# A two-layer diffusion backbone on one core: alternating block order, resident rope tables, and work moved between stages

## The chip, the cores and the metric

The kernel runs on 1 core of one Trainium2 chip. The metric is the device time of one execution in microseconds (us), lower is better. The time before is 1805.17 us, the median of 3 runs (1799.14 to 1805.18).

## The reference, cut to what matters

1024 latent tokens of width 1024 pass through two layers and a last RMSNorm, with 256 context tokens as extra keys; everything is float32.

```python
# layer 0: windowed attention, 16 query heads, 4 key/value heads of 128
shift, scale, gate = split(silu(c) @ ada_w[0] + ada_b[0], 3)
h = rmsnorm(x, norm_g[0]) * (1 + scale) + shift
q, k, v, z = split(h @ attn_w_in)            # 16 q, 4 k, 4 v, 16 z columns blocks of 128
q, k = rope(q, cos, sin), rope(k, cos, sin)
o = softmax([sink, q kc^T, masked q k^T]) @ [vc, v]   # |i-j| <= 128, and all 256 context keys
x = x + gate * ((o * silu(z)) @ attn_w_out)
# layer 1: convolution module, width 2048
shift, scale, gate = split(silu(c) @ ada_w[1] + ada_b[1], 3)
h = rmsnorm(x, norm_g[1]) * (1 + scale) + shift
a, gl, z = split(h @ conv_w_in + conv_b_in, 3)
u = depthwise_conv31(a * sigmoid(gl)) + conv_dw_b
x = x + gate * ((silu(layernorm(u)) * silu(z)) @ conv_w_out)
out = rmsnorm(x) * final_g
```

## The kernel before, in words

Every float32 product is made of three fast matmuls: each operand is split into a rounded high part (a copy on ScalarE) and a low part (the difference, `split_lo`, on VectorE or GpSimd), and high x high, high x low and low x high are added up. On chip, big tiles live in 44 pages of 128 x 1024 floats (`pg`) and 6 half pages (`hp`); `hx` hands out half pages, from `hp` first and then from `pg`. A page that is freed goes to the end of a queue and is handed out again in that order; whoever writes it next waits for its last reader, DMAs among them.

The stages, with their times in the profile:

- **Start (0 to 78 us).** Modulation of layer 0, the normalized input (`Hh`, `Hl`: high and low, 8 tiles of 128 x 1024 each), first projections.
- **Attention (78 to 930 us).** 128 steps, one for each head and block of 128 queries. A step issues the scores of the next step (`scores`), then `fill(n)`, then `pv` when one is queued, then `transposes`. TensorE works in program order. `fill` puts projection matmuls between the softmax steps so that TensorE has work while VectorE, ScalarE and GpSimd make the softmax; `quota(h, qb)` is the running count of such matmuls at each step (`HEAD0` for head 0, then sums for groups of heads). Small steps that follow a matmul are put off by a number of such matmuls (`soon(n, fn)`).
- The fill consists of the gate of head 0 (`job_gate`), context keys and values (`job_ctx`), and **pairs** (`job_pair`): two columns of weights of 128 (for instance q and z of one head) times all 1024 tokens, by the seven products of the Strassen-Winograd scheme in place of eight, each product 12 matmuls of 512 columns, 84 a pair, 18 pairs. `PairStream` loads a pair's two weight blocks, makes their sums and splits them, two products ahead. `sums` makes the sums of the input once (S1 to S4). S4 and S3 stay on chip; S1 and S2 are written to device memory (`sd`) and streamed back in each pair, four tiles of 512 KB each (`stream`, `hdone`). The pair stream has 11 pages of its own (`PW`). A pair's results need `finish`: rope for q and k (`rope_late`: two DMAs swap the halves of the head, and cosine and sine tables are loaded from device memory each time), the gate for z, a transpose for v.
- In the same steps run two jobs by the way. `ada_rest` makes the gate of layer 0 and all of layer 1's modulation: 16 chunks of 256 columns, 8 multiply-adds of 128 x 256 on VectorE each, the weights loaded 128 KB at a time into two buffers (`dww_raw`, `wsum_raw`), the sum kept beside the mask (`mask_page`). `low_parts` loads `conv_w_out` in 32 pieces, makes the low parts on ScalarE and GpSimd, and stores them (`wolC`).
- **Attention's output projection (930 to 1080 us)**, `proj_attn`: its weights are loaded, copied on ScalarE, and their low parts made on GpSimd; after each of its 32 steps `bgA` runs small jobs.
- **Convolution (1080 to 1585 us)**, and **last projection (1585 us to the end)**, `proj_out`: 32 steps of 24 matmuls; `w_load` loads the weight and its low part from `wolC`, `w_split` makes the high part. The second half of the layer norm runs between its steps (`bgB`).

Instruction order on VectorE, ScalarE, GpSimd and the DMA queue of SyncE (SP) is set by a planner outside the kernel from the dependencies and its own costs; each engine then works in that order.

Of the kernel before, what the change touches and what calls it, by code (L numbers as in the profile page):

```python
# [36 lines left out]
PW = 11  # L37
KEPT = 12
ROPE_AT = 12
HEAD0 = (30, 36, 36, 36, 36, 28, 28, 28)  # L40
# [109 lines left out]
def backbone_kernel(  # L150
# [185 lines left out]
    for key, src in (("k", 0), wk[0]), (("q", 0), wcol(0)), (("v", 0), wv[0]), (("z", 0), wcol(AW + 2 * KW)):  # L336
        add_chunk(key, src)
# [3 lines left out]
    wsA = WStream(chunks, nraw=4, lo_eng=lambda i: V if i < 4 or i % 2 else G)  # L341

    pairs = []
    for h in range(1, NH):
# [6 lines left out]

    pw = []

    class PairStream:
# [6 lines left out]
        def load(self):  # L361
            if self.nl >= 2 * len(pairs):
                return
            i, c = divmod(self.nl, 2)
            r = pw[0].alloc(F32, [2, 512], "wraw")
            SY.dma_start(out=r.rearrange("p a (b c) -> p (a b) c", c=P), in_=column(pairs[i][c]))
            self.raw[(i, c)] = r
            self.nl += 1

        def halves(self, src, i, b, then=None):  # L370
            t = pw[0].alloc(F32R, [2, 512], "whl")
# [10 lines left out]
        def split(self):  # L382
# [6 lines left out]
            r1, r2 = self.raw.get((i, 0)), self.raw[(i, 1)]  # L389

            def drop(c):
                pw[0].free(self.raw.pop((i, c)))
                self.load()

            if b == 0:
                self.halves(r1[:, 0], i, b)
                self.t[i] = t = pw[0].alloc(F32, [2, 512], "wt")
                tt(V, t[:, 0], r2[:, 1], r2[:, 0], ALU.subtract)
            elif b == 1:
                t = self.t[i]  # L400
                self.halves(t[:, 0], i, b)
                tt(V, r2[:, 0], r2[:, 0], r1[:, 0], ALU.subtract)
                tt(V, t[:, 1], r2[:, 1], r2[:, 0], ALU.subtract)
            elif b == 2:
                self.halves(r1[:, 1], i, b)
                tt(V, r1[:, 0], r1[:, 1], self.t[i][:, 1], ALU.subtract)
            elif b == 3:
                t = self.t.pop(i)
                self.halves(t[:, 1], i, b, lambda: pw[0].free(t))
            elif b == 4:  # L410
                self.halves(r1[:, 0], i, b, lambda: drop(0))
            elif b == 5:
                self.halves(r2[:, 1], i, b)
            else:
                self.halves(r2[:, 0], i, b, lambda: drop(1))
# [9 lines left out]
        def done(self, n):  # L425
            pw[0].free(self.hl.pop(n))
# [376 lines left out]

    def ada_rest():
        todo = [(l, c0) for l, c0 in [(0, 2048 + 256 * i) for i in range(4)] + [(1, 256 * i) for i in range(12)]]
        todo = [(l, c0, kt) for l, c0 in todo for kt in range(KT)]

        def load(i):
            l, c0, kt = todo[i]
            SY.dma_start(out=ada_raw[i % 2], in_=ada_w[l, kt * P:(kt + 1) * P, c0:c0 + 256])  # L810
# [3 lines left out]
        for i, (l, c0, kt) in enumerate(todo):  # L814
# [3 lines left out]
            if kt == 0:  # L818
                after(V.tensor_scalar(out=acc, in0=raw, scalar1=cs[:, kt:kt + 1], scalar2=None, op0=ALU.mult))
                for b in range(2):  # L820
                    col = (c0 - 2048 if l == 0 else 1024 + c0) // P + b
                    bs = slice(b * P, b * P + P)
                    stt(acc[:, bs], ident, abt[:, col:col + 1], acc[:, bs], ALU.mult, ALU.add)
            else:
                after(stt(acc, raw, cs[:, kt:kt + 1], acc, ALU.mult, ALU.add))
            yield "sum" if kt == KT - 1 else None
# [3 lines left out]
            if c0 >= 2048:  # L830
                PE.matmul(o[0:1, 0:256], ones[:, 0:1], acc_a, start=True, stop=True)
                row = hx.alloc("grow")
                V.tensor_copy(row[0:1, 0:256], o[0:1, 0:256])
                SY.dma_start(out=gd[l][:, c0 - 2048:c0 - 1792], in_=row[0:1, 0:256])
                soon(2 * KEPT, lambda row=row: hx.free(row))
            else:
                for b in range(2):
                    PE.matmul(o[:, b:b + 1], acc_a[:, b * P:b * P + P], ones[:, 0:1], start=True, stop=True)
                V.tensor_copy(mod1[:, c0 // P:c0 // P + 2], o[:, 0:2])
            yield  # L840

# [6 lines left out]
    wolC = dr.tile([2, NK, P, 2, 512], F32, tag="wolC", name="wolC")  # L848

# [3 lines left out]

    def low_parts():

        his = hx.alloc("lhi")
        hi = his.bitcast(F32R)
        for m in range(2):
            for kk in range(NK):
                for b in range(2):  # L860
                    raw = hx.alloc("low")
                    SY.dma_start(out=raw, in_=pair_rows(Wp, m, kk)[:, b])
                    yield
                    after(act(hi, raw, AF.Copy), anchor_a)
                    after(split_lo(G, raw, raw, hi), anchor_p)
                    yield
                    SY.dma_start(out=wolC[m, kk][:, b], in_=raw)
                    soon(KEPT, lambda raw=raw: hx.free(raw))
                    yield
        hx.free(his)  # L870
# [169 lines left out]
    def early_proj():  # L1040
        pg.free(*Hh, *Hl, *s4)
# [38 lines left out]
    def rope_late(e, half, d, then, queue):  # L1080
# [14 lines left out]
        def high_low():  # L1095
            hx.free(w, ct, st)
# [4 lines left out]
        def low(hi, lo):  # L1101
            split_lo(G, lo, e, hi)
            soon(KEPT, lambda: hx.free(e))
            if then:
# [5 lines left out]
    def rope(o, half, d, ropes=None, e=None, then=None):  # L1110
        sl = slice(half * 512, half * 512 + 512)
        if e is not None:
            return rope_late(e, half, d, then, SY)
        e = hx.alloc("rope")
        act(e, o, AF.Copy)
        if soon_on[0]:
            return rope_late(e, half, d, then, A)
# [36 lines left out]
    def finish(kind, n, half, o, d=None, ropes=None, e=None):  # L1154
# [7 lines left out]
        if kind in "qk":  # L1162
# [3 lines left out]
            rope(o, half, d, ropes, e, then)  # L1166
# [65 lines left out]
    def job_gate():  # L1232
        i = cidx[("z", 0)]
        wc = wsA.need(i)
        for half in range(2):
            o = ps_g()
            yield from gemm_half(wc, half, o)
            wsA.load()
            wsA.split()
            finish("z", 0, half, o)  # L1240
        wsA.done(i)
        for k in range(4):
            drive(sums(k), 1 + S_EVERY * k)
# [5 lines left out]
    def job_ctx(kind, g):  # L1249
        i = cidx[(kind, g)]  # L1250
        wc = wsA.need(i)
        wsA.load()
        o = ps_g()
# [14 lines left out]
        if (kind, g) == ("v", NG - 1):  # L1268
            for c in Hc:
                pg.free(*c)  # L1270
            pw.append(pg.part(PW))
            for _ in range(2):
                wsP.load()
            wsP.ahead(1)
            for k in range(4):
                stream(0, k)

    s4, win, ready = [], {}, set()
    ORDER = ("A11", "S3", "A12", "S2", "A22", "S4", "S1")
    STREAM = ("S2", "S1")  # L1280

    def sums(k):

        f, g = (pg.alloc(F32, [2, 512], "sf") for _ in range(2))
        for t, i, eng in ((f, k, V), (g, k + 4, G)):
# [7 lines left out]
        new = {n: pg.alloc(F32R, [2, 512], n) for n in ("S2", "S4", "S1")}  # L1293
        s4.append(new["S4"])
        dst = {n: (t[:, 0], t[:, 1]) for n, t in new.items()}
        dst["S3"] = Hh[k][:, 512:1024], Hl[k][:, 512:1024]
        for n, src in (("S3", f[:, 1]), ("S2", f[:, 0]), ("S4", g[:, 0]), ("S1", g[:, 1])):
# [1069 lines left out]
```

## Time and profile before

| what | value |
|---|---|
| median of 3 runs | 1805.17 us |
| the profiled execution, its own time | 1802.11 us |
| its span, first to last instruction | 1800.3 us |
| TensorE (PE) busy | 1682.3 us, 93% |
| VectorE (DVE) busy | 1374.4 us, 76% |
| GpSimd (POOL) busy | 1012.5 us, 56% |
| ScalarE (ACT) busy | 919.4 us, 51% |
| moved by DMA | 347.40 MB |

A matmul is counted as busy to its modelled end, and these overlap, so that a group's sum of durations is more than its share of the engine's time; the views by window count overlapped time once. Nearly all instructions go through short helper functions, so the line given (L144) says nothing; tiles are told by name. `name<-a,b` is written tile, read tiles. A name belongs to the first user of a half page, so `oz_page` or `sin_page` may hold another thing later.

### The profile page before, as it was taken

To read this page: it belongs to the slowest core of one execution; us is meant where nothing else is said; L and a number is where in the kernel's file an instruction comes from. 1 tells how busy PE (TensorE), PEld (TensorE's weight loads), DVE (VectorE), ACT (ScalarE), POOL (GpSimd) and SP (SyncE) were. 2 spreads that over 40 slices of the span, in tenths; PEclk is the share of its full clock that TensorE was granted. 3 is DMA by queue.
4 is the path that set the end of the run, shared out by engine and by line. 5 is a ranking of instruction groups with operands and counts; after the bars stand their busy time and mean duration, and the time that the engine had idled before them with its cause. 6 is when DMAs were issued, how large, how long until landed. Compare 5 with 4: busy or idle time off the path is not lost.

```text
span 1800.3 us, 24912 instructions
## 1 busy us (share of the span) xinstructions
PE 1682.3 (93%) x8221; PEld 1400.5 (78%) x8221; DVE 1374.4 (76%) x2337; ACT 919.4 (51%) x1649; POOL 1012.5 (56%) x778
## 2 busy tenths in 40 slices
PE   9986999978989989898889999999999999999998
PEld 6775777867778777776778888888888888878886
DVE  5995778976778777777832638999999999976833
ACT  6643554544455444444533435565656655466732
POOL 0464556654556555564634566799988998320300
PEclk9988999998999999999999999999999999999999
DMA  9457789966798779977645443110111112177891
GB/s 377 149 174 263 240 281 338 328 226 212 256 312 297 251 239 303 293 260 236 211 150 177 152 149 121 35 60 24 59 59 51 67 48 82 65 250 236 285 336 68
DMA packets 158498, 347.40 MB, mean 193 GB/s; under 512 B 16938, under 2 KB 43874, under 8 KB 158368
## 3 DMA queue, kind: packets, MB, share of 16 engines
q1 hardware_dynamic: 155168, 340.56, 56.2%
q10 hardware_dynamic: 3200, 5.25, 1.0%
q8 instruction: 65, 1.06, 0.2%
q14 instruction: 65, 0.53, 0.1%
HBM read 281.50 MB, written 53.75 MB: 186 GB/s over the span
## 4 chain that ended last, share of the span: by engine, by line
PE 62%; DVE 14%; DMA 13%; issue 4%; POOL 2%; ACT 2%; SPq 1%; ACTq 0%; DVEq 0%; POOLq 0%
PE psg L144 27%; PE pso L144 18%; PE pss L144 17%; DMA wraw_page<-in_k_win_dram 3%; DMA sw_page<-sd 2%; DVE mask_page L144 2%; DVE ptlo L144 2%; DVE p L144 2%; DVE sf_page L144 1%; DMA dww_raw<-in_ada_w_dram 1%; DMA rope_half<-rope_half 1%; DVE oz_page L144 1%; DMA wo_page<-in_attn_w_out_dram 1%; DVE wraw_page L144 1%; SPq L144 1%
## 5 line engine op out<-in xcount | busy, mean ns | idle before, releaser
L144 POOL TENSOR_TENSOR odd_half<-odd_half,prod_half 128x513 f32<-128x513 f32 (+2 forms) x252 | 315.8, 1261 | 27.4 <-ACT prod_half L144 14.4
L144 ACT ACTIVATE prod_half<-ubuf,dww 128x513 f32<-128x513 f32 (+2 forms) x252 | 167.1, 676 | 133.0 <-POOL odd_half L144 126.8
L144 POOL TENSOR_SCALAR p<-p,sc 128x640 f32<-128x640 f32 (+1 forms) x128 | 120.8, 944 | 188.7 <-DVE sc L144 122.6
L144 PE MATMUL psg<-hh_page,whl_page 128*128 128x512 f32 x576 | 193.4, 401 | 7.3 <-ACT oz_page L144 6.6
L144 PE MATMUL psg<-h2h_page,whi_page 128*128 128x512 f32 x464 | 181.8, 392 | 0.0
L144 PE MATMUL psg<-h2h_page,wlo_page 128*128 128x512 f32 x464 | 180.6, 389 | 0.0
L144 PE MATMUL psg<-h2l_page,whi_page 128*128 128x512 f32 x464 | 180.6, 389 | 0.0
L144 ACT ACTIVATE p<-p,sc 128x641 f32<-128x641 f32 (+1 forms) x128 | 102.9, 804 | 137.9 <-DVE sc L144 122.4
L144 DVE SCALAR_TENSOR_TENSOR pss<-ubuf,wsum,pss 128x512 f32<-128x512 f32 (+3 forms) x270 | 173.0, 676 | 0.3
L144 DVE SCALAR_TENSOR_TENSOR pss<-ubuf,dww,pss 128x512 f32<-128x512 f32 (+3 forms) x270 | 172.8, 676 | 0.2
L144 POOL TENSOR_TENSOR wlo_page<-wraw_page,whi_page 128x1024 fp32r<-128x1024 f32 (+1 forms) x38 | 88.8, 2341 | 115.0 <-ACT whi_page L144 77.6
L144 ACT ACTIVATE pthi<-pss 128x512 fp32r<-128x512 f32 (+2 forms) x144 | 86.7, 613 | 99.6 <-PE pss L144 94.2
L144 PEld LDWEIGHTS psg<-hh_page,whl_page 128*128 128x128 f32 x576 | 109.9, 194 | 29.0 <-ACT oz_page L144 7.0
L144 DVE TENSOR_TENSOR ptlo<-pss,pthi 128x512 fp32r<-128x512 f32 (+2 forms) x144 | 101.2, 712 | 30.6 <-ACT pthi L144 29.9
L144 ACT ACTIVATE woh_page<-wo_page 128x1024 fp32r<-128x1024 f32 x63 | 66.6, 1057 | 107.6 <-DMA wo_page<-in_conv_w_out_dram 44.8
L144 PE MATMUL pss<-kh_page,q_page 128*128 128x384 f32 (+1 forms) x256 | 97.8, 382 | 23.4 <-ACT q_page L144 9.8
L144 PE MATMUL pso<-h2h_page,whi_page 128*128 128x512 f32 x304 | 118.3, 389 | 0.0
L144 PE MATMUL pso<-h2l_page,whi_page 128*128 128x512 f32 x304 | 118.3, 389 | 0.0
L144 PE MATMUL pso<-h2h_page,wlo_page 128*128 128x512 f32 x304 | 118.3, 389 | 0.0
L144 PE MATMUL psg<-hl_page,whl_page 128*128 128x512 f32 x288 | 115.4, 401 | 0.0
L144 PE MATMUL pss<-ident,p 128*128 128x128 f32 x608 | 90.3, 278 | 22.8 <-DVE ptlo L144 11.2
L144 POOL TENSOR_TENSOR wol_page<-wo_page,woh_page 128x512 fp32r<-128x512 f32 x62 | 83.2, 1365 | 50.2 <-ACT woh_page L144 26.7
(536 smaller groups left out, 4714.7 us busy)
## 6 DMA issues: line engine op xcount, KB each, us to landing
sw_page<-sd SPq DMA_DIRECT2D x144, 512.0 KB, 6.1
wraw_page<-in_k_wconv_dram SPq DMA_DIRECT2D x48, 512.0 KB, 3.2
wraw_page<-in_k_win_dram SPq DMA_DIRECT2D x46, 512.0 KB, 5.0
wo_page<-in_attn_w_out_dram SPq DMA_DIRECT2D x32, 512.0 KB, 5.6
wo_page<-in_conv_w_out_dram SPq DMA_DIRECT2D x32, 512.0 KB, 9.7
wol_page<-wolC SPq DMA_DIRECT2D x32, 512.0 KB, 5.7
araw_page<-in_k_ada_dram SPq DMA_DIRECT2D x16, 512.0 KB, 10.2
dww_raw<-in_ada_w_dram SPq DMA_DIRECT2D x64, 128.0 KB, 4.5
```

The costliest lines, as they stand in the source:

```text
L144: r = f(*a, **k)
```

## The change

- **Pairs.** The order of the seven products is S1, A11, S3, S2, A12, S4, A22 in pairs of even number and A22, A11, S3, S2, A12, S4, S1 in odd ones. The tile at the end of a pair stays for the start of the next, so that only one of the two streamed tiles is loaded a pair (`stream_in`, 16 matmuls after the start, and up to 24 later while four pages or fewer are free). S2 takes the place of A22 in `Hh`, `Hl`; A22 and S1 are stored to `sd`. The bank that ends the pair changes with the order, weight sums follow it. One of four result sums goes from VectorE to GpSimd.
- **Head 1.** Its q and z are no pair: they are computed whole (`job_whole`, 48 matmuls each), so that there are 17 pairs. `sums` starts in the middle of z of head 1.
- **Pages.** The 11 pages of the pair stream are no longer set apart.
- **Rope.** The tables `cos` and `sin` stay on chip (two pages); the loads in `rope_late` are gone.
- **Fill.** `QUOTA` gives the fill for each head. Before the scores of a half head, fill goes on until rope of that half q has ended (before: until the pair had got to q of that head).
- **Modulation.** `ada_rest` keeps the gate of layer 0 (4 of 16 chunks, a step in three). Layer 1's is made in `ada_last`, three small pieces after each step of attention's output projection: 48 multiply-adds of 128 x 512, 24 loads of 512 KB. Biases are added at the end of a chunk, not by a multiply-add with the identity for each block.
- **Low parts.** `low_parts` and `wolC` are gone; `w_split` makes the low part in the last projection, two subtractions of 128 x 512 a step, on GpSimd (on VectorE for the first).

```diff
-HEAD0 = (30, 36, 36, 36, 36, 28, 28, 28)
+X_AT, X_TRIES, X_LEAVE = 16, 24, 4
+ADA_EVERY = 3
+QUOTA = (180, 236, 118, 118) + (105,) * 8 + (77, 77, 78, 78)
...
     def rope_late(...):
-        w, ct, st = (hx.alloc(n) for n in ("rope", "cos", "sin"))
+        w = hx.alloc("rope")
+        ct, st = (t[:, half * 512:half * 512 + 512] for t in (cos, sin))
         def swap():
             queue.dma_start(out=w[0:64], in_=e[64:128])
             queue.dma_start(out=w[64:128], in_=e[0:64])
-            for a, src in ((ct, k_cos), (st, k_sin)):
-                SY.dma_start(out=a, in_=src[:, half * 512:half * 512 + 512])
...
+    def stream_in(n, k, tries=X_TRIES):
+        if len(pg.free_) > X_LEAVE or not tries:
+            return stream(n, k)
+        soon(1, lambda: stream_in(n, k, tries - 1))
...
-    def hdone(i, n, k):
-        if n not in STREAM:
+    def hdone(i, b, n, k):
+        if b == 0:
+            pg.free(win.pop((n, k)))
+            soon(X_AT, lambda: stream_in(STREAM[1 - STREAM.index(n)], k))
+        if i < len(pairs) - 1:
             return
-        pw[0].free(win.pop((n, k)))
-        a = 1 - STREAM.index(n)
-        if i == len(pairs) - 1 and a == 0:
-            return
-        stream(a, k)
+        if b == 6:
+            pg.free(win.pop((n, k)))
+        elif b == 5:
+            pg.free(s4[k])
+        elif b in (2, 4):
+            at = k if b == 2 else k + 4
+            pg.free(Hh[at], Hl[at])
...
     def job_pair(i):
-        for b, n in enumerate(ORDER):
+        if i % 2:
+            a_, c_ = c_, a_
+        ends = STREAM[::-1] if i % 2 else STREAM
+        for b, n in enumerate((ends[0], "A11", "S3", "S2", "A12", "S4", ends[1])):
...
             if b == 3:
                 tt(V, zs, b_, zs, ALU.add)
+                if i % 2:
+                    tt(G, e0, e0, zs, ALU.add)
+                    finish(k1, n1, 1, None, d, e=e0)
+                else:
+                    e2 = hx.alloc("e")
+                    tt(G, e2, e0, zs, ALU.add)
+                    ended(k2, n2, 1, e2, 3, 12)
...
-        if nxt and nxt[1] == 0:
-            fill(1000, ("q", h + 1))
+        if nxt and nxt[1] % 4 == 0 and nxt[0]:
+            fill(1000, ("q", nxt[0], nxt[1] // 4))
...
-        if h:
-            next(lows, None)
...
-        for _ in range(2 if qb == 1 or qb == 6 and h % 2 else 1):
-            if adone and (adone[0] != "sum" or not did):
+        if (i % ADA_EVERY == 0 or adone[0] == "sum") and (adone[0] != "sum" or not did):
...
     def w_split(i):
-        w, wl = wst[i]
-        wh = pg.alloc(F32R, [2, 512], "woh")
+        w = wst[i]
+        wh, wl = pg.alloc(F32R, [2, 512], "woh"), pg.alloc(F32R, [2, 512], "wol")
         act(wh, w, AF.Copy)
+        for e in range(2):
+            split_lo(G if i else V, wl[:, e], w[:, e], wh[:, e])
...
     def bgA(s, kk):
+        for _ in range(3):
+            next(adal, None)
```

The new generator that runs there:

```python
def ada_last():
    todo = [(c, kk) for c in range(6) for kk in range(4)]
    for i in range(3):
        load(i)                                   # 512 KB of ada_w[1] into a page
    acc_pg = pg.alloc(F32, [2, 512], "acc")
    yield
    for i, (c, kk) in enumerate(todo):
        acc = acc_pg[:, c % 2]
        for a in range(2):
            ...                                   # acc += raw[a] * silu(c), VectorE, 128 x 512
            if a:
                pg.free(raws.pop(i)); load(i + 3)
            yield
        if kk < 3:
            continue
        yield; yield; yield
        ...                                       # TensorE sums over partitions, VectorE adds the bias
        yield
    pg.free(acc_pg)
```

More of the change, by code (lines that the diff above doesn't have):

```diff
@@ L819, in ada_rest @@
                 after(V.tensor_scalar(out=acc, in0=raw, scalar1=cs[:, kt:kt + 1], scalar2=None, op0=ALU.mult))
[L820 to L823, printed above, removed]
             else:
                 after(stt(acc, raw, cs[:, kt:kt + 1], acc, ALU.mult, ALU.add))
+            if kt == KT - 2:
+                row = bias_row(c0, 256)
             yield "sum" if kt == KT - 1 else None
@@ L829, in ada_rest @@
             o = ps_o(0)
[L830 to L835, printed above, removed]
-            else:
-                for b in range(2):
-                    PE.matmul(o[:, b:b + 1], acc_a[:, b * P:b * P + P], ones[:, 0:1], start=True, stop=True)
-                V.tensor_copy(mod1[:, c0 // P:c0 // P + 2], o[:, 0:2])
+            PE.matmul(o[0:1, 0:256], ones[:, 0:1], acc_a, start=True, stop=True)
@@ L1165, in finish @@
                 d, then = staged(kd[n], half)
-            rope(o, half, d, ropes, e, then)
+            rope(o, half, d, ropes, e, then, lambda: finished.add((kind, n, half)))
             return None
@@ L1674, in backbone_kernel @@
     for i, (h, qb) in enumerate(steps):
-        if (h, qb) == (NH - 2, 5):
-            while next(lows, "end") != "end":
-                pass
         if h == NH - 2 and qb > 4:
-            if wsP.ns == 7 * len(pairs) and pw[0].free_ is not pg.free_:
-                pw[0].back()
             next(projA)
```

288 lines of the change are left out of this document (162 added, 126 removed).

## The prediction

> **What bounds the kernel now.** I read the page first, then the busy times by stage, then who ended TensorE's idle time, then the chain of waits in the attention stage. Columns of the windows: busy us (x instructions) of each engine, mean granted TensorE clock, share of the DMA engines, GB/s.
>
> ```profile
> span 1800.3 us, 24912 instructions
> PE 1682.3 (93%) x8221; PEld 1400.5 (78%) x8221; DVE 1374.4 (76%) x2337; ACT 919.4 (51%) x1649; POOL 1012.5 (56%) x778
> ```
> ```profile
> 78.00:930.00 852.00, 750.56 (x3903) 633.64 (x3904) 652.14 (x1115) 407.85 (x880) 478.90 (x384) 0.94 0.77 254
> 268.00:363.00 95.00, 90.32 (x490) 76.25 (x488) 81.42 (x140) 48.97 (x109) 59.39 (x47) 1.00 0.97 332
> 363.00:426.00 63.00, 48.14 (x232) 40.87 (x232) 42.59 (x69) 27.70 (x58) 31.02 (x26) 0.89 0.62 202
> 930.00:1080.00 150.00, 150.00 (x684) 124.55 (x684) 59.69 (x93) 53.39 (x77) 80.83 (x58) 1.00 0.51 168
> 1080.00:1585.00 505.00, 504.60 (x2244) 417.30 (x2242) 482.79 (x783) 293.85 (x422) 406.46 (x300) 1.00 0.19 64
> 1585.00:1800.00 215.00, 205.39 (x932) 170.76 (x932) 126.61 (x234) 113.19 (x184) 38.08 (x26) 0.99 0.69 237
> ```
>
> TensorE is the bound, and after 930 us it hardly waits: nothing can be won there but fewer matmuls, and the change takes none away there. Attention (78 to 930 us) is the only stage with time to give: TensorE is idle for 852.00 - 750.56 = 101.4 us, and its clock is 0.94 in the mean. How much of this could come back is shown by its own best stretch: from 268 to 363 us it ran 490 matmuls in 95 us at clock 1.00, 5.16 a us. 3903 at that rate take 757 us, so the whole loss is about **95 us**. The bad stretch right behind it (363 to 426 us) ran 232 in 63, 3.7 a us.
>
> What ended TensorE's idle time in that stage (us in total, times, longest):
>
> ```profile
> PE pso L144 <- DVE ptlo L144: 16.4, 12, 4.0
> PE pss L144 <- DVE ptlo L144: 11.6, 14, 3.6
> PE pss L144 <- POOL p L144: 9.5, 6, 2.9
> PE pss L144 <- DVE sc L144: 9.0, 14, 1.5
> PE pss L144 <- ACT q_page L144: 8.1, 3, 6.5
> PE psg L144 <- ACT oz_page L144: 6.6, 1, 6.6
> PE pss L144 <- POOL q_page L144: 4.8, 3, 2.1
> PE pss L144 <- DVE q_page L144: 1.4, 1, 1.4
> ```
>
> Two kinds: the softmax comes late (ptlo, p, sc), and the rotated q comes late at the start of a head (q_page: 8.1 + 4.8 + 1.4 = 14.3 us). Neither has heavy work of its own. Why they are late is told by the chain of waits, by line for the stage and then in the pieces that end in the 6.6 us wait for oz_page:
>
> ```profile
> by line: PE psg L144 10.5%; PE pso L144 10.0%; issue 8.7%; PE pss L144 7.7%; DMA sw_page<-sd 4.1%; DVE mask_page L144 3.9%; DVE ptlo L144 3.8%; DVE p L144 3.7%; DMA wraw_page<-in_k_win_dram 3.6%; DMA dww_raw<-in_ada_w_dram 2.1%; DMA rope_ha
> ```
> ```profile
> 339.52 1.27 POOL zl_page L144
> 340.81 6.63 DMA wolC<-zl_page
> ...
> 349.09 7.78 DMA oz_page<-zl_page
> ...
> 356.95 3.74 DMA wolC<-oz_page
> ...
> 360.70 1.75 POOL whl_page L144
> 362.45 1.67 POOL oz_page L144
> ```
>
> The first store of a low part (6.63 us) keeps a half page that VectorE wants next, the rope's swap (7.78 us) follows, another store of a low part comes before GpSimd's work, and TensorE stands. Engines work in order, so one late DMA holds the softmax that is queued behind it.
>
> **The change part by part.** Most of it takes things out of the attention stage. Their rows there (the low parts' by one representative name each):
>
> ```profile
> sw_page<-sd SPq DMA_DIRECT2D x144, 512.0 KB, 6.1
> sin_page<-in_k_sin_dram SPq DMA_DIRECT2D x14, 256.0 KB, 4.2
> L144 DVE SCALAR_TENSOR_TENSOR mask_page<-wsum_raw,cs,mask_page 128x256 f32<-128x256 f32 x63 | 52.2, 828 | 1.9 <-DMA wsum_raw<-in_ada_w_dram 1.6
> L144 DVE SCALAR_TENSOR_TENSOR mask_page<-dww_raw,cs,mask_page 128x256 f32<-128x256 f32 x48 | 35.4, 738 | 10.8 <-DMA dww_raw<-in_ada_w_dram 10.8
> L144 DVE SCALAR_TENSOR_TENSOR mask_page<-ident,abt,mask_page 128x128 f32<-128x128 f32 x30 | 21.6, 759 | 0.0
> L144 DVE TENSOR_SCALAR mask_page<-dww_raw,cs 128x256 f32<-128x256 f32 x15 | 10.4, 696 | 0.0
> 78.00:930.00 852.00, 20.03 (x32) 44.70 (x32) 0.94 0.77 254
> 78.00:930.00 852.00, 8.97 (x48) 4.88 (x48) 223.36 (x284) 0.94 0.77 254
> L144 POOL TENSOR_TENSOR wol_page<-wo_page,woh_page x62: 1260/1292/2276, 852.4 to 1060.4; 128x512 fp32r<-128x512 f32 x62
> ```
>
> (The two window rows are those of the tile lhi_half, ACT and POOL, and of mask_page, PE, PEld and DVE; the last row has min/median/max in ns.)
>
> - *Streamed tiles.* One tile a pair in 17 pairs, 68 loads in place of 144: 76 x 0.524 = 39.8 MB less. A22's store is more of the same 512 KB a tile, in place of S2's.
> - *Rope tables.* 36 half heads x 2 x 0.262 = 18.9 MB less. Two pages are held; against them, two half pages for each rope under way and the low parts' two or three are free.
> - *Low parts.* 32 loads and 32 stores of 0.262 MB = 16.8 MB, 20.03 us of ScalarE and 44.70 us of GpSimd leave.
> - *Modulation.* A quarter of the multiply-adds stays, none with the identity: VectorE loses 0.75 x (52.2 + 35.4 + 10.4) + 21.6 = 95 us of its 652.14. 96 loads of 0.131 MB, 12.6 MB, leave.
> - *Traffic and issue.* Together 88 MB of the stage's 254 GB/s x 852 us = 216 MB, and 308 DMAs fewer on SP's queue, where stores and loads wait in order.
> - *Sums in a pair.* On VectorE one of four result sums a pair goes (to GpSimd, some 1.3 us x 17 = 22 us by the wol_page row, so GpSimd is still 23 us lighter); odd pairs make one weight sum more. VectorE: about nothing.
> - *Matmuls.* Whole q and z of head 1 take 96 in place of 84: 12 more at 505/2244 = 0.225 us, **+2.7 us**.
> - *Waiting for q.* Fill goes on until the low part of that q half is issued. So the 14.3 us of waits for q are filled with matmuls that are due later anyway; the scores queued behind come a few matmuls later.
>
> What comes back of the 95 us? From below: the streamed tiles' chain, 4.1% of 852 x 76/144 = 18 us, modulation's sums on VectorE, 3.9% x 95/119.6 = 26 us, its loads, 2.1% x 0.75 = 13 us, with the 14.3 us for q make 72 us. This is too much, as behind each stands the next (wraw_page's loads at 3.6%, rope's swaps, p and ptlo), which come sooner only as far as traffic and VectorE's queue allow. Bounds: nothing, and 95 us. I take two thirds of the 72, **-48 us**, which is half of the loss.
>
> The Trainium skill (TensorE: Matmul & The Clock Gate, Part 1: The HAM clock gate) says that the array runs at half clock after an idle window of some 3.4 us, and until it has been busy as long. The clock of 0.89 behind the long wait, against 1.00 in the best stretch, agrees; by that rule 0.06 x 852 = 51 us would come back on top of the idle time. The rate of 5.16 was measured at clock 1.00, so my 95 us hold it already.
>
> **Later stages.** The mask_page row has 8.97 us of TensorE for 48 small matmuls, three quarters of which go to the output projection, where TensorE has no idle time (150.00 of 150.00). They cost 6.7 us there and free at most as much in attention, where part of it was covered by waits: **+3.3 us** (0 to 6.7). VectorE's 48 multiply-adds of 512 columns cost 48 x 0.83 x 2 = 80 us at most by the 256-column row, beside 59.69 of 150 us busy; cover is there, without it TensorE's sums wait. DMA adds 12.6 MB to 168 GB/s x 150 us = 25 MB. SP's queue holds the stores of the gate behind VectorE's sums, and weight loads behind them; these run two steps ahead.
>
> In the last projection, GpSimd gets 62 subtractions of 1.29 us median, 80 us, beside 38.08 of 215. A step of 24 matmuls is 5.4 us; two subtractions are 2.6 us, at the worst of the row 4.6. The attention's projection does just this at 150.00 of 150.00 busy. But here the layer norm shares both engines:
>
> ```profile
> L144 POOL TENSOR_TENSOR v_page<-v_page,zsl_half x20: 1282/1307/1741, 1590.0 to 1698.1; 128x512 f32<-128x512 f32 x20
> L144 DVE TENSOR_TENSOR v_page<-v_page,zsl_half x11: 678/695/1794, 1598.0 to 1696.9; 128x512 f32<-128x512 f32 x11
> L144 DVE TENSOR_TENSOR gs_page<-v_page,gs_page x40: 677/687/1793, 1609.1 to 1719.0; 128x512 fp32r<-128x512 f32 x40
> ```
>
> VectorE's 0.69 us becomes 1.79 beside GpSimd. If all 51 of these met it, VectorE had 56 us more, still below 215. In the layer norm's last 22 us or so GpSimd's ten multiplications take some 15, and four steps of low parts would add 10 to 18: up to 12 us late. I take **+2 us** (0 to 12). The 16.8 MB of low-part loads that go there free nothing, as TensorE does not wait for them.
>
> The Trainium skill (SBUF — State Buffer, SBUF: two separate sides) speaks against this move: a GpSimd instruction and a VectorE instruction with two SBUF inputs take a shared pair of ports whole, and the other blocks. The 1.79 us against 0.69 agree. By that rule alone the last projection could lose the 12 us at most, and the sum would be 10 us higher.
>
> **Sum.** -48 + 2.7 + 3.3 + 2 = -40 us on the profiled execution's 1802.1 us: **1762 us**. The median of 1805.17 is 3 us above that execution, which is within the spread shown.
>
> **The rivals.**
> - *Only the bound is moved.* The softmax's own chain (p, sc, ptlo: 16.4 + 11.6 + 9.5 + 9.0 = 46.5 us of TensorE's idle time) stays as it is, and what was removed was only first in line. For it: DMA at 0.97 in the best stretch, so traffic alone does not stop TensorE. Against: VectorE loses a seventh of its work. The stage returns 0 to 22 us: 1788 to 1810.
> - *All comes back.* Each stretch runs like 268 to 363: -95 + 2.7, so 1710 to 1730. Against: that stretch had VectorE at 86%, and heads without such luck are most.
> - *Slower: the one streamed tile comes late.* It is asked for 16 to 40 matmuls after the pair's first product and needed after 72. Fill runs 1800 matmuls in 852 us, 0.47 us each, which leaves 15 to 26 us for a landing of 6.1 us; a page whose last reader is late could eat that, and then TensorE, in program order, stands, 17 times. It decides from 40/17 = 2.4 us a pair; at a full landing it is 17 x 6.1 = 104 us, so 1866. Against: the margin is 9 us or more.
>
> **How the numbers follow.** Forecast (the stage returns 23 to 75 us, 1732 to 1787) 0.64; all comes back 0.12; only the bound is moved 0.16; slower by a late tile or in the last projection 0.08. The range from 1722 to 1803 leaves out the lower half of the second and what lies above no change, some 0.17 in all. A measurement of this kernel can tell 0.5%, 9 us, from no change. Faster (below 1796): 0.64 + 0.12 + half of the third, 0.84; same 0.08; slower 0.08.
>
> **What would show it.** Right: attention ends at about 885 us with TensorE idle for some 55 us there, traffic near 150 GB/s, waits for q_page near nothing, the clock at 0.97; the projections keep TensorE busy throughout. Wrong: idle time as before with ptlo and p as releasers (first rival), TensorE waiting for sw_page at a pair's last product (third), or woh_page, wol_page and gs_page as releasers after 1585 us.

## The result, and the profile after

The changed kernel takes 1751.63 us (median of 4 runs, 1749.19 to 1752.54) against 1803.49 us for the kernel before (4 runs): a ratio of 0.971, 95% interval 0.969 to 0.974. The forecast was 1762 us, 1722 to 1803. The profiled execution has a span of 1747.4 us, 52.9 less than before; here it is by stage. Attention begins with VectorE's first instruction on the scores and ends with the last product of probabilities and values; the output projection ends where its last matmul with `ozh_page` starts, and the last projection begins with the first matmul that reads `gs_page`.

| stage | before | after | difference | forecast |
|---|---|---|---|---|
| start | 78.8 | 76.9 | -1.9 | 0 |
| attention | 844.8 | 765.8 | **-79.0** | -45.3 (-48 + 2.7) |
| attention's output projection | 159.8 | 175.8 | **+16.0** | +3.3 |
| convolution | 532.0 | 535.2 | +3.2 | 0 |
| last projection | 184.9 | 193.7 | **+8.8** | +2 |
| sum | 1800.3 | 1747.4 | -52.9 | -40 |

So the sum came out 13 us from the forecast because two errors went opposite ways: the attention stage gave 34 us more, and the later stages took 23 us more. The windows of three stages before (attention, output projection, last projection), then busy times and four stages of after (columns of the windows as above):

```profile
78.00:923.60 845.60, 744.16 (x3870) 628.87 (x3871) 650.15 (x1110) 405.82 (x879) 473.13 (x374) 0.94 0.77 255
923.60:1083.80 160.20, 160.20 (x732) 132.49 (x732) 64.28 (x106) 57.37 (x82) 87.52 (x71) 1.00 0.52 169
1615.30:1800.00 184.70, 177.24 (x806) 147.27 (x804) 103.76 (x190) 93.23 (x155) 26.48 (x17) 0.99 0.69 236
```
```profile
PE 1665.7 (95%) x8229; PEld 1391.3 (80%) x8229; DVE 1342.3 (77%) x2234; ACT 904.7 (52%) x1618; POOL 1077.9 (62%) x823
76.90:842.60 765.70, 713.04 (x3840) 610.61 (x3839) 544.13 (x952) 391.56 (x847) 440.67 (x357) 0.97 0.50 165
842.60:1018.90 176.30, 169.29 (x770) 137.23 (x769) 113.05 (x161) 57.53 (x83) 95.97 (x71) 0.99 0.65 218
1018.90:1553.60 534.70, 531.70 (x2355) 439.91 (x2354) 506.47 (x824) 313.69 (x452) 423.13 (x312) 0.99 0.21 70
1553.60:1747.40 193.80, 179.24 (x805) 148.71 (x804) 128.68 (x188) 91.54 (x152) 114.50 (x77) 0.97 0.46 143
```

In attention, TensorE's idle time fell from 845.60 - 744.16 = 101.4 us to 765.70 - 713.04 = 52.7 us, and its clock rose from 0.94 to 0.97; VectorE has 106 us less to do, and traffic went from 255 to 165 GB/s. In the output projection TensorE, which had no idle time, has 7.0 us of it, and 9.1 us more busy time. In the last projection GpSimd's 26.48 us have become 114.50. Who ended TensorE's idle time in attention, after:

```profile
PE pss L145 <- DVE ptlo L145: 14.5, 10, 3.8
PE pss L145 <- POOL p L145: 9.5, 5, 4.6
PE pso L145 <- DVE ptlo L145: 6.9, 4, 4.0
PE pss L145 <- DVE sc L145: 4.6, 6, 1.2
PE pss L145 <- POOL q_page L145: 3.4, 2, 2.2
```

The waits for q went from 14.3 to 3.4 us; those for the softmax (ptlo, p, sc) from 46.5 to 35.5.

### The profile page after: what moved, and what is told of

It is laid out like the page before. It is cut to its first block, busy times and chain, and to the rows that moved or that the text cites. A ratio compares the mean times of both kernels' runs of the same rounds, so it can differ in the third digit from the quotient of the medians.

```text
span 1747.4 us, 24154 instructions
## 1 busy us (share of the span) xinstructions
PE 1665.7 (95%) x8229; PEld 1391.3 (80%) x8229; DVE 1342.3 (77%) x2234; ACT 904.7 (52%) x1618; POOL 1077.9 (62%) x823
## 4 chain that ended last, share of the span: by engine, by line
PE 67%; DVE 14%; DMA 9%; issue 4%; POOL 3%; ACT 2%; SPq 1%; DVEq 0%; ACTq 0%; POOLq 0%
PE psg L145 29%; PE pso L145 21%; PE pss L145 17%; DMA wraw_page<-in_k_win_dram 2%; DVE acc_page L145 1%; DVE wt_page L145 1%; DVE ptlo L145 1%; DVE p L145 1%; DMA araw_page<-in_ada_w_dram 1%; DVE sf_page L145 1%; POOL whl_page L145 1%; DVE whl_page L145 1%; DVE pss L145 1%; SPq L145 1%; DVE v_page L145 1%
## 5 line engine op out<-in xcount | busy, mean ns | idle before, releaser
L145 POOL TENSOR_TENSOR wol_page<-wo_page,woh_page 128x512 fp32r<-128x512 f32 x124 | 183.6, 1508 | 96.4 <-ACT woh_page L145 64.8
L145 POOL TENSOR_SCALAR p<-p,sc 128x640 f32<-128x640 f32 (+1 forms) x128 | 113.2, 884 | 164.7 <-DVE sc L145 117.0
L145 PE MATMUL psg<-hh_page,whl_page 128*128 128x512 f32 x408 | 136.4, 397 | 0.4 <-DVE stage_page L145 0.4
L145 ACT ACTIVATE woh_page<-wo_page 128x1024 fp32r<-128x1024 f32 x63 | 65.6, 1053 | 95.7 <-DMA wo_page<-in_attn_w_out_dram 46.5
L145 PE MATMUL pss<-woh_page,gs_page 128*128 128x512 f32 (+1 forms) x352 | 111.1, 387 | 0.0
L145 PEld LDWEIGHTS pss<-ident,p 128*128 128x128 f32 x608 | 72.0, 142 | 41.8 <-POOL p L145 17.1
```

Source lines behind the costliest of these rows:

```text
L145: r = f(*a, **k)
```

## The experiments

Four theories were put up. **A**: late transfers and small work queued on in-order engines hold the softmax up; each part of the change gives its share. **B**: only VectorE's queue matters, so the modulation's sums give most. **C**: pair order, fill counts and the new mark for q give the gain, and the rest only makes room. After the first runs came **D**: the pairs help because the streamed loads no longer run together with the rope's swap; and its rival **E**: less work and traffic in sum.

One caution for all of them: the planner orders the whole kernel anew for each edit. Where an edit touched only the last projection of the changed kernel, attention came out 5 to 8 us longer. Differences of a stage below some 8 us are therefore not put down to an edit. The stages come from one profiled execution of each kernel, too.

### The parts, one after the other

Four kernels go from before to after in steps. The first has only the low parts moved (the diffs here are cut to the lines that matter):

```diff
-                next(lows, None)        # low_parts in attention, wolC
+        for e in range(2):              # in w_split
+            split_lo(G if i else V, wl[:, e], w[:, e], wh[:, e])
```

> The kernel before with one part alone: low parts of conv_w_out made in the last projection (no low_parts, no wolC). Attention loses 16.8 MB, 45 us of GpSimd, 20 us of ScalarE; the last projection gets 80 to 95 us of GpSimd. Theory A (late transfers and queued small work both stop the softmax, so each part taken out gives back its share): attention 20 us shorter, last projection 9 us longer, total about -11 us. Theory B (only VectorE's queue matters): attention 5 us shorter, total about +4 us. Theory C (pair order, fill counts and the mark for q give the gain, the other parts only make room): attention unchanged, total +9 us.

The second is the kernel before with only the modulation moved (`ADA_EVERY = 3` and `ada_last`):

> The kernel before with one part alone: layer 1's modulation in the output projection, a quarter of ada_rest in attention. Attention loses 95 us of VectorE and 12.6 MB; the output projection gets 16 us longer as it did with the whole change. Theory A: attention 25 us shorter, total about -9 us. Theory B: attention 45 us shorter, total about -29 us. Theory C: attention 0 to 8 us shorter, total +8 to +16 us.

The third is the first, with the rope tables kept on chip:

```diff
-        w, ct, st = (hx.alloc(n) for n in ("rope", "cos", "sin"))
+        w = hx.alloc("rope")
+        ct, st = (t[:, half * 512:half * 512 + 512] for t in (cos, sin))
```

> As b_low, with the rope tables kept on chip as well (18.9 MB and 72 loads fewer). Theory A: attention 20 us shorter than in b_low, total about -31 us against before. Theory B: as b_low, +4 us. Theory C: as b_low, +9 us.

The fourth is the third with the modulation moved too, so that only pairs, head 1, pages and fill are missing:

> As b_lr, with layer 1's modulation in the output projection as well: all of the change but the pairs, head 1, pages and fill. Theory A: attention 55 to 65 us shorter, later stages 28 us longer, total about -32 us; the pairs are worth the last 20 us. Theory B: attention 50 us shorter, total -22 us. Theory C: attention 0 to 10 us shorter, total +20 us, and the pairs are worth all of the gain.

Measured (before: 1802.18 us; stages from the traces):

| kernel | us | ratio, 95% | attention | output projection | last projection |
|---|---|---|---|---|---|
| before | 1802.18 | | 844.8 | 159.8 | 184.9 |
| low parts | 1802.94 | 1.001 [0.999, 1.003] | 835.7 | 159.8 | 194.8 |
| low parts, tables | 1800.30 | 0.9995 [0.998, 1.002] | 830.3 | 159.8 | 194.1 |
| modulation | 1784.57 | 0.991 [0.987, 0.994] | 811.8 | 177.0 | 184.7 |
| low parts, tables, modulation | 1787.79 | 0.993 [0.990, 0.995] | 795.0 | 177.6 | 194.8 |
| after | 1751.63 | 0.971 [0.969, 0.974] | 765.8 | 175.8 | 193.7 |

Down the attention column: low parts -9, tables -5, modulation -35 (alone -33), pairs and what goes with them -29: -79. For the first two A had expected -20 each, B -5 and nothing; for the modulation alone A had -25 and B -45; so neither has all the sizes, and the tables' 5 us lie within what a new order does. The two moved parts pay in the stages to which they go: the low parts +10, which is all that they gain; the modulation +17 of its 35. C falls, since more than half of the stage's gain is there without pairs or fill. Tables alone on the kernel before, or the low parts back in the changed one, weren't run.

The profiled execution of the fourth kernel was the fastest of its ten (1781.05 us, median 1787.79). By the medians of whole runs the four steps are +0.8, -2.6, -12.5 and -36.2 us, so the -35 may be up to some 7 us too large and the -29 as much too small. The modulation alone, -33, does not rest on that execution.

### The modulation: VectorE's side or the transfers?

The kernel before, with layer 1's loads and small matmuls in place, without its multiply-adds and bias adds:

```diff
-            if kt == 0:
+            if l:
+                pass
+            elif kt == 0:
```

> The kernel before with layer 1's modulation loads and small matmuls as they are, and its 96 multiply-adds of 128 x 256 and their 24 additions of the bias left out (the shift, scale and gate of layer 1 are then not computed). If VectorE's work is the price (theory B): attention 30 us shorter as in the kernel that moves the modulation, total about 1772 us. If VectorE's waits for the loads are the price (theory A): 5 us, total about 1798 us.

1766.76 us, ratio 0.980 [0.977, 0.982]. Windows of attention and output projection, of this kernel and then of the one with the modulation moved:

```profile
79.00:888.90 809.90, 730.52 (x3868) 623.16 (x3867) 564.13 (x990) 406.50 (x879) 466.14 (x374) 0.95 0.81 267
888.90:1049.20 160.30, 160.30 (x734) 132.57 (x733) 61.70 (x106) 57.28 (x82) 87.24 (x71) 1.00 0.51 169
```
```profile
78.00:889.80 811.80, 723.90 (x3828) 616.86 (x3827) 577.24 (x979) 404.10 (x877) 477.61 (x374) 0.95 0.76 253
889.80:1067.20 177.40, 170.34 (x769) 138.37 (x769) 110.08 (x153) 57.60 (x84) 97.93 (x71) 0.98 0.63 214
```

The stage is as short (-35 us) with all the loads still there and the traffic at 267 GB/s. So the transfers themselves cost nothing that can be seen, and what the modulation cost in attention was on VectorE: B is right for this part. But the run does not part the multiply-adds from VectorE's waits for their loads, which went with them. These waits in attention were 10.8 + 1.6 us before; here there is left:

```profile
DVE mask_page L144 <- DMA dww_raw<-in_ada_w_dram: 1.8, 1, 1.8
DVE mask_page L144 <- DMA wsum_raw<-in_ada_w_dram: 1.1, 1, 1.1
```

The second lines of the windows show the price of the move by itself: 177.4 us in the output projection, against 160.3.

### The new mark for q

The changed kernel with the old mark, so that the scores wait only until the pair has got to q:

```diff
-            rope(o, half, d, ropes, e, then, lambda: finished.add((kind, n, half)))
+            finished.add((kind, n, half))
+            rope(o, half, d, ropes, e, then)
```

> The changed kernel with the old mark: a head's scores may be issued as soon as the pair has handed over its q, not when rope's low part is issued. If the waits for q that went were won by the mark (the prediction's 14.3 us): total 10 to 14 us longer, TensorE waiting for q_page again. If the new fill counts keep q early by themselves: no change.

1754.09 us, ratio 0.973 [0.971, 0.976]; attention 765.2 us, and the wait for q is the same to the last digit:

```profile
PE pss L145 <- POOL q_page L145: 3.4, 2, 2.2
```

The mark gave nothing. That the waits for q went has another cause: with low parts, tables and modulation moved they were still 10.4 us, so most of it lies in the last step, and the next experiment shows a part.

### The traffic, put back

The changed kernel with 88 MB of copies between buffers in device memory, about what the change took out of attention. The first try had them free of any dependency:

```diff
+        src = k_wconv[i % 48].rearrange("p k c -> p (k c)")
+        SY.dma_start(out=extra[i % 8], in_=src)
+        if qb < 5:
+            SY.dma_start(out=extra[8 + i % 8][:, 0:512], in_=src[:, 512:1024])
```

> The changed kernel with the traffic put back as dummy copies in device memory, 208 in 128 attention steps, 88 MB, on SP's queue; nobody waits for them. If traffic and the lateness of other transfers were what the change won (theory A): attention 30 us longer or more, total 1785 us or more. If it is the work in the engines' queues and the order of the pairs (theories B, C): within 8 us of the changed kernel, 1750 to 1760 us.

1880.59 us, ratio 1.044 [1.042, 1.046], but not for the asked reason: with nothing to wait for, the copies were put at the kernel's beginning.

```profile
0.00:420.00 420.00, 297.62 (x1525) 245.56 (x1526) 207.23 (x365) 159.00 (x310) 125.31 (x105) 0.83 0.97 347
420.00:970.70 550.70, 514.19 (x2781) 440.97 (x2780) 391.45 (x697) 284.10 (x623) 313.89 (x263) 0.98 0.52 170
```

That is the price of full DMA engines (0.97 for 420 us, TensorE busy 71%), 39 us of it before the first scores. The second try ties each copy to the step's split of the probabilities:

```diff
+        if anchor:
+            paced(SY.dma_start(out=extra[i % 8], in_=src))
+            if qb < 5:
+                paced(SY.dma_start(out=extra[8 + i % 8][:, 0:512], in_=src[:, 512:1024]))
```

> The changed kernel with 88 MB of copies between buffers in device memory added in the attention stage, what the change took out there, each held back until its step's probabilities have been split, so that they lie spread over the 128 steps (in the earlier run with free copies all of them ran in the first 420 us). Theory A (traffic holds the in-order engines up): attention is 25 us or more longer, swaps and loads land later all through. Theory B (work, not traffic): attention under 10 us longer, about 1760 in all. The copies also stand in SP's queue and can hold up loads behind them: where only those are late (waits for wraw_page, sw_page), it is the queue, not the traffic.

1777.76 us, ratio 0.987 [0.982, 0.992]. The window of attention, TensorE's waits for q there, and how long SP's queue stood for the splits:

```profile
76.90:871.00 794.10, 721.15 (x3841) 618.14 (x3840) 537.97 (x952) 392.00 (x847) 449.08 (x360) 0.96 0.78 269
```
```profile
PE pss L145 <- ACT q_page L145: 8.2, 3, 4.1
PE pss L145 <- POOL q_page L145: 7.6, 5, 2.8
SPq L145 <- DVE ptlo L145: 128.9, 60, 7.2
```

The same work on every engine (VectorE 537.97 against 544.13 us), the traffic of before (269 GB/s), and the stage is 28 us longer, with waits for q of 15.8 us in place of 3.4. So A holds as well: with the copies q is late again, mark or no mark, and the stage pays for them. A copy reads and writes device memory while most of what was removed were loads, so 28 us may be on the high side. A rival is left: the copies stood in SP's queue and held it for 128.9 us (1.4 in after), so that a DMA behind them can be late by the queue and not by the traffic. Against it: TensorE had no wait for `sw_page` or `wraw_page`, VectorE and ScalarE waited for `wraw_page` 18.1 us in place of 20.2, and the rope's swaps on that queue were issued 0.4 us in the mean after the last write to their source (0.2 in after). It is not excluded for the other DMAs there.

### Do streamed loads collide with the rope's swap?

The swaps on ScalarE's queue, 170 to 830 us, in the kernel with low parts, tables and modulation moved, then in after, then with the paced copies (the last number is the median time to landing, in us):

```profile
rope_half<-rope_half ACTq DMA_DIRECT2D x10, 128.0 KB, 5.7
```
```profile
rope_half<-rope_half ACTq DMA_DIRECT2D x12, 128.0 KB, 2.3
```
```profile
rope_half<-rope_half ACTq DMA_DIRECT2D x12, 128.0 KB, 4.4
```

These medians rest on one, one and two landings that the traces could tell. Under all its tile names the swap has 6, 4 and 11 on that queue, with medians of 7.0, 2.5 and 4.4 us. Counted by start times on both queues, two DMAs a swap, 58 of 68 DMAs of the first had a streamed load issued in the 6 us before or 2 us after them (64 of 64 before the change), 12 of 68 after. For theory D the changed kernel asks later for its tile:

```diff
-X_AT, X_TRIES, X_LEAVE = 16, 24, 4
+X_AT, X_TRIES, X_LEAVE = 44, 0, 4
```

> The changed kernel with its one streamed tile a pair asked for 44 matmuls after the pair's first product, without looking at free pages (before this: 16, and up to 24 later). Theory D (collision): the 29 us that the pairs and head 1 gave came because the loads of 512 KB no longer run at the same time as the rope's swap of 128 KB, which then lands in 2.3 us in place of 5.7 to 7.7. Asked for at 44, the four loads fall on the swap again: swaps land in 5 to 7 us, VectorE and GpSimd wait for them in order, attention is 15 to 25 us longer, 1767 to 1777 us in all. Theory E (less work and traffic in sum): the tile has the same number of loads and still comes before its use at 72, so attention stays within 8 us of the changed kernel's 766, about 1752 in all. A third outcome, the tile late: TensorE waits for sw_page itself, which neither explains.

1743.41 us, ratio 0.968 [0.964, 0.971]; attention 757.9 us. It made no collision: 14 of 68 had a load beside them, and the swap landed in the same time (four landings in this row).

```profile
rope_half<-rope_half ACTq DMA_DIRECT2D x12, 128.0 KB, 2.3
```

So it says nothing against E and doesn't test D. The other side of it, in the kernel without the new pairs, uses the rotated halves later:

```diff
-ROPE_AT = 12
+ROPE_AT = 16
```

> The kernel before with low parts, tables and modulation as in the changed one, but the old pairs (1788 us), and here the rotated q and k put together 16 matmuls after the swap is asked for in place of 12, some 2 us later. Theory D (collision): part of the late swap is covered, VectorE and GpSimd wait less for it, attention falls by 5 to 15 us from 795, in all 1773 to 1783. Theory E: the swap was only one of many waits, and attention stays within 8 us, 1780 to 1796; against it as well stands that q itself comes 2 us later at a head's start.

1792.11 us, ratio 0.994 [0.992, 0.996], 4 us above the 1787.79 of the kernel with 12; attention 803.4 us against 795.0 in the latter's fastest execution. Waits of VectorE and GpSimd for the swap, under all its tile names, from 170 to 830 us, were 51.2 and 75.2 us (51.3 and 81.2 with 12), so 4 matmuls more hardly covered it. The paced copies speak against D too: there the waits for the swap were 43.8 and 48.9 us (37.6 and 51.9 in after), about the same in sum, and the stage lost 28 us all the same. D is not shown, and its remedy failed.

### The last projection

Low parts in the changed kernel: on VectorE for steps 8 to 17 only, then for all steps, in both as one subtraction of 128 x 1024:

```diff
-            split_lo(G if i else V, wl[:, e], w[:, e], wh[:, e])
+        split_lo(V, wl, w, wh)
```

> The changed kernel with the low parts of steps 8 to 17 of the last projection made on VectorE in one instruction of 128 x 1024, not on GpSimd. If the 7 us wait for the layer norm's root is due to GpSimd's subtractions holding VectorE's two-input work: the wait goes to below 2 us and the total is 6 to 9 us shorter. If VectorE is simply too full there: no change or longer.

> The changed kernel with all low parts of the last projection on VectorE, one subtraction of 128x1024 a step, none on GpSimd. If GpSimd's hold of the shared ports is what slows the layer norm there (a stall of 7 us for the factor r, gs_page sums of 1.7 in place of 0.69 us), the last projection falls from 194 to some 186 us and the whole to 1743 to 1747. If VectorE, which then has 31 x 1.4 = 43 us more beside 129 of 194, becomes the one that is late, the stage stays at 194 or grows, with ptlo's place taken by wol_page in TensorE's waits. Differences of up to 8 us in attention are the order that the planner chose.

For the steps 8 to 17: 1753.15 us, ratio 0.973 [0.971, 0.975]; for all: 1752.57 us, 0.973 [0.969, 0.976]. The last projection took 192.0 and 190.8 us in place of 193.7, and in both, attention came out longer (773.6 and 770.7), so neither beats the changed kernel. The largest loss there is one stall, in the stage's middle. Some rows of after (start, duration), up to the factor r on which TensorE waits:

```profile
1605.19 6.73 DVE L145 TENSOR_TENSOR gs_page<-v_page,gs_page 128x512 fp32r<-128x512 f32 x4
1606.36 10.01 POOL L145 TENSOR_TENSOR wol_page<-wo_page,woh_page 128x512 fp32r<-128x512 f32 x6
1611.84 1.74 DVE L145 TENSOR_TENSOR x_page<-x_page,fg_page 128x512 f32<-128x512 f32 x1
1613.57 0.16 DVE L145 RECIPROCAL rr<-sq 128x4 f32<-128x4 f32 x1
1613.65 1.60 DVE L145 TENSOR_TENSOR gs_page<-v_page,gs_page 128x512 fp32r<-128x512 f32 x1
1615.17 1.21 DVE L145 SCALAR_TENSOR_TENSOR rq<-rr 128x4 f32<-128x4 f32 x1
1616.62 0.16 DVE L145 SCALAR_TENSOR_TENSOR r<-rq,rr 128x4 f32<-128x4 f32 x1
1616.92 1.41 PE L145 MATMUL pso<-ident,r 128*128 128x128 f32 x5 [6.95 <-DVE r L145]
```

And the same place in the kernel before:

```profile
1670.13 0.18 DVE L144 RECIPROCAL rr<-sq 128x4 f32<-128x4 f32 x1 [0.27 <-ACT sq L144]
1670.34 0.16 DVE L144 SCALAR_TENSOR_TENSOR rq<-rr 128x4 f32<-128x4 f32 x1
1670.74 0.16 DVE L144 SCALAR_TENSOR_TENSOR r<-rq,rr 128x4 f32<-128x4 f32 x1
```

GpSimd runs six subtractions without a pause, and each 128 x 512 operation of VectorE beside it takes 1.6 to 1.7 us. Six of them stand before r in VectorE's order, and TensorE stands for 6.95 us. With steps 8 to 17 on VectorE no GpSimd instruction runs beside the last operations ahead of r, and those of 128 x 512 take 0.6 to 0.7 us; but low parts of 1.2 us now stand among them, and TensorE waits for 4.6 us (below 2 was expected):

```profile
1618.01 1.21 DVE L145 TENSOR_TENSOR wol_page<-wo_page,woh_page 128x1024 fp32r<-128x1024 f32 x1
1619.14 1.28 DVE L145 TENSOR_TENSOR gs_page<-v_page,gs_page 128x512 fp32r<-128x512 f32 x2
1620.44 1.19 DVE L145 TENSOR_TENSOR wol_page<-wo_page,woh_page 128x1024 fp32r<-128x1024 f32 x1
1622.84 2.05 PE L145 MATMUL pso<-ident,r 128*128 128x128 f32 x8 [4.56 <-DVE r L145]
```

With every low part there the wait is gone, and the next one shows, for an input of another small product:

```profile
PE pso L145 <- ACT qa_half L145: 2.6, 1, 2.6
```

The stage got 2.9 us shorter by it, not 8 as expected. So GpSimd beside VectorE stretches what stands ahead of r, but VectorE's order alone can make the same wait, and the hold is not shown to be the cause of the whole 8.8 us.

## Why the prediction came out as it did

- **Right:** attention as the only stage with time to give. It ended at 842.6 us (885 was said), with 52.7 us of idle time (55), 165 GB/s (150), clock 0.97 (0.97) and waits for q of 3.4 us (near nothing). The streamed tile is never late: TensorE has no wait for `sw_page`, and asking at 44 in place of 16 costs nothing, so that rival was as far off as its margin said.
- **The step that failed first: "This is too much, as behind each stands the next" and, after it, "I take two thirds of the 72, -48".** The stage returned 79.0 + 2.7 = 82 us, of which at most 6.7 are the small matmuls that left: 75 to 82 us of the 95 us loss, at the upper end of the forecast case's 23 to 75 or between it and the rival in which all comes back. By the stage alone that rival was as near; the later stages brought the sum back into the forecast case, which is luck. The terms came back almost whole: the modulation's sums and VectorE's waits for their loads, 26 + 13 = 39 us in the text, measured 33 to 35 us; streams and q, 18 + 14.3, stand against -29 for pairs, head 1, pages and fill (up to some 7 more by the medians). That is some 64 of the 72, so the discount was wrong. Low parts and tables, listed among the parts but without a term, gave -9 and -5 on top. Inside these sums the split is not shown: no run parts the sums from the waits for their loads, and q was put down to the mark. Why what stood behind each did not take its place stays open; that less work on VectorE brings the next waits sooner too would explain it, but is argued, not shown.
- **The mark for q** was a wrong mechanism: the waits went without it and came back with the copies.
- **The output projection: "+3.3 us (0 to 6.7)" was +16.** The term was sized by the small matmuls' busy time. With the modulation alone moved the stage takes 177.4 us (160.2 before), so the loss belongs to it. In the trace of after, its 36 small matmuls there take 10.1 us by their own durations, which overlap, and TensorE stands where its small products wait for VectorE, on which multiply-adds stand ahead (five of 0.75 us among the small operations before the `xn_page` shown). First the tile's rows, then one such wait, then windows of TensorE around it (busy us, clock, DMA share, GB/s):

```profile
L145 DVE SCALAR_TENSOR_TENSOR acc_page<-araw_page,cs,acc_page x42: 740/752/1776, 846.3 to 954.7; 128x512 f32<-128x512 f32 x42
L145 PE MATMUL pso<-ones,acc_page x32: 164/250/250, 859.5 to 924.2; 128*128 128x1 f32 x32
L145 PE MATMUL pso<-acc_page,ones x4: 590/590/591, 952.1 to 979.8; 128*1 128x512 f32 x4
```
```profile
937.96 1.26 PE L145 MATMUL pso<-ident,xn_page 128*128 128x128 f32 x5 [2.15 <-DVE xn_page L145]
```
```profile
934.70:938.10 3.40, 1.25 (x8) 1.00 0.29 92
938.10:941.50 3.40, 3.40 (x11) 0.50 0.68 197
```

By gaps between matmul starts, stalls and half clock make 11.5 us of the 16 (0.7 before), and the small matmuls themselves the rest. The text's "cover is there, without it TensorE's sums wait" named this and priced it at nothing.
- **The last projection: "+2 (0 to 12)" was +8.8**, inside its bounds and in part by the mechanism named, VectorE and GpSimd beside each other; the other part is the order of VectorE's queue, which makes such a wait without GpSimd (4.6 us for r). Matmul starts there show 9.0 us of gaps and half clock, 0.8 before; the one long wait is that for r. The weights' low parts were never late, which is what the steps of 5.4 us against 2.6 had looked at; the small operation in between was not looked at. The Trainium skill (SBUF — State Buffer, SBUF: two separate sides) says that either instruction holds the shared pair of ports until it ends and the other blocks. The 1.7 against 0.69 us, and the 1.21 against 0.16 us of an operation on 128 x 4 elements, agree.
- **Open:** the 3 us in the convolution and the 2 us at the start, which lie within what a new order does; what of the pairs' 29 us is traffic, and what is head 1, pages or fill. The 28 us of the copies stand for the traffic of low parts, tables, streams and modulation together, and hold what SP's queue added.

**A better version?** The tile asked for at 44 gave 1743.41 us, but its interval (0.964 to 0.971) meets that of the changed kernel (0.969 to 0.974), and 8 us of attention is what a new order can do. It is the fastest seen, not shown to be faster. The modulation's sums, with the waits for their loads, cost some 35 us in attention and 17 in the output projection; whether a stage hides them fully was not tried.

## What to carry to other kernels

Work that is moved off a busy stage must be priced where it lands: ask there which small result of the same engine TensorE waits for next, and how many long instructions stand ahead of it, not only whether the engine has time in sum. Shares of the chain of waits added up to 72 us here; the runs gave some 64 for the same items, so a discount "for the next in line" needs a reason of its own, and parts without a term (14 us here) need one. To part a line's work from its loads, a run must keep the waits: leaving out the work left out the waits for its loads as well. When an experiment adds work to spread over a stage, tie it to the stage's steps, or an ordering tool may put all of it at the beginning.

## What the runs showed of the hardware

- A VectorE operation on 128 x 4 elements with two inputs took 1.21 us beside GpSimd's subtractions, 0.16 us without them; operations of 128 x 512 with two inputs took 1.6 to 1.7 against 0.69 us.
- A swap's DMA of 128 KB on chip, on ScalarE's queue, landed in 2.2 to 4.0 us where no streamed load was issued beside it (four landings, in after), and in 5.7 to 7.8 us where on the average 3.3 were (six landings, in the kernel with low parts, tables and modulation moved). The whole traffic differed as well (171 and 222 GB/s from 170 to 830 us).
- TensorE's clock fell to one half after a stretch of 3.4 us in which it was busy for 1.25 us, so without being idle throughout (the windows above). The Trainium skill (TensorE: Matmul & The Clock Gate, Part 1: The HAM clock gate) names an idle window of some 3.4 us; the length agrees, and this one was over a third busy.
